# Gates of two retention heads as jobs of seven products ahead of the retention, and output projections moved into the next head

## The chip, the cores and the metric

The kernel runs on one core of one Trainium2 chip. The metric is the device time of one execution in microseconds (us); the time before is the median of three runs. PE is TensorE (matmul), DVE is VectorE, ACT is ScalarE, POOL is GpSimd, SP is SyncE, which issues most of the DMAs.

## The reference

One inference step of a two-layer decoder on 512 prompt tokens and 8 x 4 sample tokens, together T = 544 columns. The kernel keeps activations transposed, so D_MODEL = 1024 is eight tiles of 128 partitions. Layer 0 mixes with a gated short convolution, layer 1 with multi-scale retention; each is followed by a SwiGLU feed-forward.

```python
def retention_mixer(x, s0, pos, w_in, gn_g, w_out):
    z = x @ w_in                       # x: rmsnorm of the residual
    q, k, v, g = jnp.split(z, ...)     # widths 1024, 1024, 2048, 2048; 4 heads
    q = rotary(q, pos); k = rotary(k, pos) * (HEAD_DK ** -0.5)
    o, S = retention_chunkwise(q, k, v, s0)
    of = (o - mean(o)) * lax.rsqrt(var(o) + GN_EPS)       # per head
    out = (jax.nn.silu(g) * (of * gn_g)) @ w_out
    return out, S

# a layer
x = x + mixer(rmsnorm(x, norm_mix[i]))
x = x + swiglu(rmsnorm(x, norm_ffn[i]), w_gate, w_up, w_down)
```

A head has 256 key and 512 value dimensions, so a head's gate is four blocks of 128 rows (n = 0 to 3), and its output projection multiplies a 512 x 1024 part of `w_out` and adds to all eight residual tiles.

## The kernel before

**Split products.** Every float32 operand is split into a high part and the rest (`split`, lines 186 to 190: a copy on ACT, a subtraction on DVE), and each product is made as three matmuls: high by high, high by rest, rest by high. `project` (L173) makes one 128-row output block of 544 columns in two halves of 272 (HT): per 128 rows of the contraction 3 x 2 matmuls. Weights come by `load_piece` (512 KB, on SP) into a pool of three buffers and are split into `wh` and `wl`.

**Feed-forward.** `ffn` makes gate and up in jobs (`class Job`): two output blocks by two token halves by two halves of the contraction are a 2 x 2 product of blocks, which is made with seven products in place of eight, from sums of weight blocks (`weights7`, L434 to L437 on DVE, with accumulating DMAs on POOL in `mixed`, L422) and sums of activation blocks (`operands_left`, `operands_rest`, tiles `oh` and `ol`). The results are gathered in tiles `gu` (`summed`). `run` goes through the jobs: each one's weights are prepared a job ahead. The down projection (`down`) adds to the residual tiles `x` (`residual`, L269), and for layer 0 it makes the split input `xh`, `xl` of the next layer at the end (`split_x`), and sums squares on ACT and POOL (`square_sum`). `rms_scale` turns the sums into R, the reciprocal norm per token (the norm's scale is applied to results).

**Retention.** After the feed-forward's pools are closed, `qk_first` makes the first head's two key blocks and its first query block, scales and rotates them (`qk_rotate`; cosine and sine are held in `sqacc` and `sqlast`). Then, for each head h:

- `value`: 96 + 96 products of 512 columns, with the splits of queries and keys (`qk_split`), sample scores (L1090) and key transposes in the middle;
- `gate_project` for n = 0 to 3, set between the state products (`state`) and the scores (`scores`): `project`, then R on DVE (L1011), Silu and the gain on ACT;
- `sample_outputs` and `states_update` for four pieces of the sample state S (1 MB each, three buffers; loaded at L1106, updated at L1137, written at L1138), `inner` products, `normalized`, and `gated_pair`, which multiplies the gate tile in place;
- the next head's keys and queries (`qk_start`, `qk_project`) between these;
- `out_project` (heads 0 and 1): splits the gated tiles (`gated_parts`) and makes 8 x 24 matmuls. Head 2's projection is made within head 3 (`held_parts`, `held_project`), together with head 3's own (`last_project`).

Tiles that share a tag in a pool share memory, and a later one waits until the earlier one has been read. The order on each engine is set by a scheduler that works from the written order and its own estimates; `tc.issue_after` pins single steps. PSUM has two double banks (`mm`) and four single banks (`sm`).

Of the kernel before, what the change touches and what calls it, by code (L numbers as in the profile page):

```python
# [12 lines left out]
P = 128  # L13
D = 1024
KT = D // P
# [23 lines left out]
MADE = [0, 4, 2, 6, 3, 7, 1, 5]  # L39
RD = [(r, dt) for r in range(2) for dt in range(2)]  # L40
# [7 lines left out]
def hybrid_decode_kernel(ctx: ExitStack, tc: tile.TileContext, a: dict, o: dict):  # L48
# [408 lines left out]
    class Job:  # L457
# [3 lines left out]
        def __init__(self, srcs, oh, ol, sw, take):  # L461
            self.srcs, self.oh, self.ol, self.sw, self.take = srcs, oh, ol, sw, take

        lead = False
# [5 lines left out]
        def product(self, out, which, first):  # L470
            wh, wl = self.w[which]
            at, n = OPERAND[which], len(self.oh)
            for k in range(n):
                c = slice(k * P, (k + 1) * P)
                for i, (w, b) in enumerate(((wh, self.oh), (wh, self.ol), (wl, self.oh))):
                    last = nc.tensor.matmul(  # L476
                        out, w[:, c], b[k][:, at, :],
                        start=(first and k == 0 and i == 0), stop=(k == n - 1 and i == 2),
                        skip_group_check=True,
                    )  # L480
                if which not in (5, 6, 2):
                    with tc.issue_after(last.ins):
                        next(self.weave, None)
# [6 lines left out]
        def middle(self):  # L490
            for which in (5, 6) if self.lead else (6, 5):
# [3 lines left out]
                else:  # L495
                    self.c = bank()[:, :HT]
                    self.product(self.c, 5, True)
            self.b = bank()[:, :HT]
            self.product(self.b, 2, True)
            self.take("c11", self.b)  # L500
# [10 lines left out]
    def run(jobs, after, steps):  # L511

        jobs[0].lead = True
# [30 lines left out]
    def ffn(layer, next_gain):  # L544
        with ExitStack() as c1:
# [5 lines left out]
            ohl = [  # L551
                [(lp if i == KP - 1 else one).tile([P, 7, HT], F32R, tag=f"{t}{i}", name=nm(t)) for t in ("oh", "ol")]
                for i in range(KP)
            ]
            oh, ol = zip(*ohl)
# [26 lines left out]
            def gate_up(m):  # L582
# [17 lines left out]
                def up(what, src):  # L600
# [5 lines left out]
                    elif what == "c12":  # L606
# [5 lines left out]
                        [a["ffgu"][layer, 2 * j + q] for j in (m, m + HJ)], oh, ol, sw,  # L612
# [66 lines left out]
            run(jobs, after, steps)  # L679
# [5 lines left out]
            if layer == 1:  # L685
                final(last, group_acts(last), group_weights, fp, tp)

# [83 lines left out]
    ffn(0, lambda kt: g_mix(1, kt))  # L771


    with ExitStack() as c2:
        wide("m")
        vp = c2.enter_context(tc.tile_pool(name="rtv", bufs=1, reuse_waits="tile"))
        tp = c2.enter_context(tc.tile_pool(name="rt", bufs=2, reuse_waits="tile"))
# [38 lines left out]
        def qk_start(h):  # L816
# [5 lines left out]
            st["rot"] = [  # L822
                tp.tile([P, 2, T], F32, tag=f"rot{w}", name=nm("rot"), bufs=1) for w in range(2)
            ]
            return st

        def qk_first(st):

            steps = rms_scale(True, [bank(), bank()])
            ws = [load_piece(a["rtqk"][0, 2 + dt], KT * P) for dt in range(2)]  # L830
            pts = [psum() for _ in ws]
            for part in (MADE[:KP], MADE[KP:]):
                for (wh, wl), pt in zip(ws, pts):
                    first = part[0] == MADE[0]
                    project(pt, wh, wl, 0, xh, xl, first, not first, ks=part, weave=iter(()) if first else steps)
            qw, qpt = load_piece(a["rtqk"][0, 0], KT * P), [bank(), bank()]
            project(qpt, *qw, 0, xh, xl, weave=steps)
            drain(steps)
            for i, t in enumerate((cos, sin)):
                nc.sync.dma_start(t, a["rope"][i])  # L840
            for which in (1, 0):
                qk_scale(st, which)
                for dt in range(2 if which else 1):
                    qk_rotate(st, which, dt, pts[dt] if which else qpt)
# [17 lines left out]
        def qk_rotate(st, which, dt, pt):  # L862
# [4 lines left out]
            if dt == 0:  # L867
                return
# [509 lines left out]
```

## Time and profile before

| | |
|---|---|
| median of 3 runs | 1461.56 us (1461.03 to 1461.72) |
| profiled execution, its own time | 1460.43 us |
| its span | 1458.4 us |
| PE busy | 1444.1 us, 10920 matmuls |
| DVE, ACT, POOL busy | 956.2, 631.3, 130.5 us |
| mean granted PE clock | 0.998 |
| DMA | 189.62 MB, 130 GB/s over the span |

The profile is one execution. A span begins with the first instruction and ends with the last; the time of an execution has some 2 us around it. In a timeline row the first number is the start in us from the span's start, the second how long the row lasts; `x` at its end counts merged instructions, and brackets give idle time before it with what ended it. In a row of groups come busy us and the mean ns of one instruction, then the idle time before them. A row of waits gives the total in us, how many waits, and the longest. Successive instructions of an engine overlap slightly in the record, so a mean duration is a little longer than the distance from one to the next.

### The profile page before, as it was taken

Reading aid. Unit: us, or ns where it says so; the run is one execution under the profiler, and the core shown is the slowest. Engines: PE = TensorE matmul, PEld = TensorE weight load, DVE = VectorE, ACT = ScalarE, POOL = GpSimd, SP = SyncE. Lnnn points to the kernel's source line nnn. Section 1 sums busy time; section 2 is a strip of 40 time slices with the busy share of each in tenths; the row PEclk is TensorE's granted clock in tenths of the full one; section 3 lists DMA queues with packets and bytes.
Section 4 is the critical chain, followed back from the end, with each engine's and each line's share of the span. In section 5 each row is a group of like instructions: output and inputs, shape, how many; then the busy total and the mean of one; then the engine's idle time right before and its main releaser. Section 6 shows DMA issues by size and latency. Waiting matters only on the chain.

```text
span 1458.4 us, 26223 instructions
## 1 busy us (share of the span) xinstructions
PE 1444.1 (99%) x10920; PEld 1374.5 (94%) x10920; DVE 956.2 (66%) x1483; ACT 631.3 (43%) x920; POOL 130.5 (9%) x171
## 2 busy tenths in 40 slices
PE   9999999999999999999999999999999999999997
PEld 9999999999999999897988988878899999999997
DVE  5644679848749656648645934855699847749654
ACT  6222467626536435242142224133376626536434
POOL 0100011101101003000000000000011101101002
PEclk9999999999999999999999999999999999999999
DMA  6222246635546435336235613723656635536432
GB/s 227 77 91 94 90 102 152 151 109 131 131 109 144 120 82 188 109 116 236 98 116 173 203 47 116 256 101 127 175 119 148 152 109 131 134 109 145 117 80 83
DMA packets 80694, 189.62 MB, mean 130 GB/s; under 512 B 7728, under 2 KB 25008, under 8 KB 80576
## 3 DMA queue, kind: packets, MB, share of 16 engines
q1 hardware_dynamic: 66576, 162.01, 34.6%
q0 software_dynamic: 13136, 24.72, 10.2%
q8 instruction: 85, 1.39, 0.4%
q10 hardware_dynamic: 864, 1.22, 0.2%
q14 instruction: 33, 0.27, 0.1%
HBM read 166.75 MB, written 21.18 MB: 129 GB/s over the span
## 4 chain that ended last, share of the span: by engine, by line
PE 92%; DVE 5%; ACT 1%; DMA 1%; POOL 1%; issue 0%; DVEq 0%; SPq 0%; ACTq 0%; POOLq 0%
PE mm L173 39%; PE sm L476 31%; PE sm L173 7%; PE sm L897 2%; PE sm L898 2%; PE sm L899 2%; PE sm L161 2%; PE sm L163 1%; PE sm L162 1%; DVE S L1137 1%; PE sm L1116 1%; PE mm L904 1%; DVE wl L189 0%; DVE x L269 0%; PE mm L1068 0%
## 5 line engine op out<-in xcount | busy, mean ns | idle before, releaser
L188 ACT ACTIVATE wh<-w 128x1024 fp32r<-128x1024 f32 (+4 forms) x139 | 129.6, 936 | 358.0 <-PE mm L173 224.5
L173 PE MATMUL mm<-xh,wh 128*128 128x272 f32 x1020 | 213.1, 290 | 1.6 <-DVE S L1137 1.0
L173 PE MATMUL mm<-xh,wl 128*128 128x272 f32 x1020 | 210.7, 289 | 0.0
L173 PE MATMUL mm<-xl,wh 128*128 128x272 f32 x1020 | 210.0, 287 | 0.1
L476 PE MATMUL sm<-oh,wh 128*128 128x272 f32 x704 | 203.4, 289 | 1.1 <-ACT g L535 0.9
L476 PE MATMUL sm<-ol,wh 128*128 128x272 f32 x704 | 202.8, 288 | 0.0
L476 PE MATMUL sm<-oh,wl 128*128 128x272 f32 x704 | 202.4, 288 | 0.0
L189 DVE TENSOR_TENSOR wl<-w,wh 128x1024 fp32r<-128x1024 f32 (+4 forms) x139 | 150.2, 1085 | 28.2 <-ACT wh L188 25.7
L173 PEld LDWEIGHTS mm<-xh,wh 128*128 128x128 f32 x1020 | 159.9, 188 | 7.3 <-DVE wl L189 3.4
L173 PEld LDWEIGHTS mm<-xl,wh 128*128 128x128 f32 x1020 | 159.6, 188 | 0.3 <-DVE xl L201 0.3
L173 PEld LDWEIGHTS mm<-xh,wl 128*128 128x128 f32 x1020 | 159.0, 188 | 0.2
L269 DVE TENSOR_TENSOR x<-x,mm 128x544 f32<-128x544 f32 x88 | 63.3, 719 | 139.8 <-PE mm L173 139.8
L476 PE MATMUL sm<-oh,h 128*128 128x272 f32 x528 | 152.2, 288 | 0.5 <-ACT oh L188 0.5
L476 PE MATMUL sm<-oh,l 128*128 128x272 f32 x528 | 151.6, 288 | 0.0
L476 PE MATMUL sm<-ol,h 128*128 128x272 f32 x528 | 151.6, 287 | 0.0
L476 PEld LDWEIGHTS sm<-oh,wh 128*128 128x128 f32 x704 | 132.2, 188 | 1.9 <-ACT g L535 1.5
L422 POOL DMA_DIRECT2D wl<-in_ffgu_dram x88 | 75.5, 858 | 641.1 <-ACT wl L421 287.4
L476 PEld LDWEIGHTS sm<-oh,wl 128*128 128x128 f32 x704 | 132.8, 189 | 0.0
L476 PEld LDWEIGHTS sm<-ol,wh 128*128 128x128 f32 x704 | 132.2, 188 | 0.2 <-DVE ol L189 0.2
L419 ACT ACTIVATE wh<-w 128x1024 fp32r<-128x1024 f32 x88 | 93.3, 1060 | 73.9 <-PE sm L476 48.7
L476 PEld LDWEIGHTS sm<-oh,h 128*128 128x128 f32 x528 | 99.4, 188 | 1.1 <-ACT oh L188 0.9
L476 PEld LDWEIGHTS sm<-oh,l 128*128 128x128 f32 x528 | 99.4, 188 | 0.0
(259 smaller groups left out, 2976.1 us busy)
## 6 DMA issues: line engine op xcount, KB each, us to landing
w<-in_ffgu_dram SPq DMA_DIRECT2D x88, 512.0 KB, 3.9
wl<-in_ffgu_dram POOLq DMA_DIRECT2D x88, 256.0 KB, 4.8
w<-in_ffdn_dram SPq DMA_DIRECT2D x96, 192.0 KB, 2.6
S<-in_rets_dram SPq DMA_DIRECT2D x16, 1024.0 KB, 7.7
out_rets_dram<-S SPq DMA_DIRECT2D x16, 1024.0 KB, 5.4
w<-in_cvin_dram SPq DMA_DIRECT2D x21, 512.0 KB, 3.4
w<-in_rtqk_dram SPq DMA_DIRECT2D x16, 512.0 KB, 3.7
w<-in_rtv_dram SPq DMA_DIRECT2D x16, 512.0 KB, 3.6
```

What stands on the lines that cost most here:

```text
L161: nc.tensor.matmul(out, lh, rh, start=start, stop=False, skip_group_check=True)
L162: nc.tensor.matmul(out, lh, rl, start=False, stop=False, skip_group_check=True)
L173: last_product[0] = nc.tensor.matmul(half(pt, hf)[:, :HT], w[:, c], act[k][:, hf * HT : (hf + 1) * HT], start=(first and k == ks[0] and i ...
L188: h = nc.scalar.activation(dh, src, AF.Copy)
L189: last_low[0] = nc.vector.tensor_sub(dl, src, dh.bitcast(F32))
L269: last_residual[0] = nc.vector.tensor_add(xk, xk, p)
L419: nc.scalar.activation(wh, w, AF.Copy)
L422: nc.gpsimd.dma_start(wl[:, n:], src[:, n:], accum_op=ALU.add)
L476: last = nc.tensor.matmul(out, w[:, c], b[k][:, at, :], start=(first and k == 0 and i == 0), stop=(k == n - 1 and i == 2), skip_group_chec ...
L897: nc.tensor.matmul(out, xh[kt][:, ts_], wh[:, cw], start=(kt == 0), stop=False)
L898: nc.tensor.matmul(out, xh[kt][:, ts_], wl[:, cw], start=False, stop=False)
L899: nc.tensor.matmul(out, xl[kt][:, ts_], wh[:, cw], start=False, stop=(kt == KT - 1))
```

## The change

1. `ffn` gets a last step, `ahead`, inside its pools. It holds what `qk_first` did up to the products (the rms scale, two key blocks and one query block of head 0), but copies the raw results to SBUF and stores them in DRAM (`qk_made`). Then it makes the gates of heads 1 and 2 (`AHEAD`) in four jobs of seven products, two blocks each, with operands for the four sums only (products 1, 2 and 3 read `xh` and `xl`), and stores the finished gates in DRAM (`gate_made`). Stores are issued by ACT.
2. `qk_loaded` loads keys and query of head 0 back, with the decay table `gt` and the rope tables, and scales and rotates them; the second query block is made as before.
3. Heads 1 and 2 have no `gate_project`. In its four places (`fill`) they make the output projection of the head before, two residual tiles each (`held_project`). Its split operands (`held_parts`) are made within `value` and lie in the tiles `gt`, `rot1` and one of two tiles of four blocks that change places from head to head (`swapped`). The gate is loaded from DRAM behind the last of the four.
4. `out_project` is gone; heads 0, 1 and 2 end after the next head's queries. Head 3 is as before.
5. `Job` takes its operands by a function and the order of its middle products by a list; some tiles move to a pool of their own (`rtq`).

```diff
+AHEAD = (1, 2)
...
-        def __init__(self, srcs, oh, ol, sw, take):
+        def __init__(self, srcs, operand, sw, take):
...
-    ffn(0, lambda kt: g_mix(1, kt))
+    qk_made = [dram.tile([P, 2, T], F32, tag=f"qk{w}", name=nm("qkm")) for w in range(2)]
+    gate_made = {h: dram.tile([P, 4, T], F32, tag=f"g{h}", name=nm("gm")) for h in AHEAD}
+
+    def ahead(tp, fp, sw, operand_tiles):
+        wide("m")
+        steps = rms_scale(True, [bank(), bank()])
...
+        def off(which, dt, pt):
+            each(lambda p, d: nc.scalar.activation(d, p, AF.Copy), pt, halves(made[which][:, dt, :]))
+            if which:
+                if dt:
+                    nc.scalar.dma_start(qk_made[1], made[1])
+            else:
+                nc.scalar.dma_start(qk_made[0][:, dt, :], made[0][:, dt, :])
...
+        sums = {}
+        for i, k in enumerate(MADE[::2]):
+            f = fp.tile([P, 4, HT], F32, tag="f", name=nm("f"))
+            for j in range(2):
+                kt = k + j * KP
+                nc.scalar.activation(f[:, 2 * j : 2 * j + 2, :], halves(x[kt]), AF.Copy, scale=g_mix(1, kt))
+            b11, b12, b21, b22 = [f[:, j, :] for j in range(4)]
+            nc.vector.tensor_sub(b11, b12, b11)
+            nc.vector.tensor_sub(b12, b22, b12)
+            nc.vector.tensor_sub(b22, b22, b11)
+            nc.vector.tensor_sub(b21, b21, b22)
+            sums[k] = operand_tiles((i + 1) % KP, 4)
+            split(*sums[k], f)
...
+                elif what == "c12":
+                    r = R.rearrange("p a b -> p (a b)").unsqueeze(1).to_broadcast([P, 2, T])
+                    nc.vector.tensor_mul(g, g, r)
+                    nc.scalar.activation(g, g, AF.Silu)
+                    for i in range(2):
+                        nc.scalar.activation(g[:, i, :], g[:, i, :], AF.Copy, scale=g_ret(h * 4 + n + i))
+                    nc.scalar.dma_start(gate_made[h][:, n : n + 2, :], g)
...
+        jobs = [gates(h, n) for h in AHEAD for n in (0, 2)]
+        jobs[0].prepare()
+        run(jobs, (2, 5, 6), lambda i: None, iter(()))
+
+    ffn(0, lambda kt: g_mix(1, kt), ahead)
...
-        def qk_first(st):
+        def qk_loaded(st):
+            loads = [
+                (st["rot"][1], qk_made[1]), (cos, a["rope"][0]), (sin, a["rope"][1]),
+                (st["rot"][0][:, 0, :], qk_made[0][:, 0, :]),
             ]
...
+        def swapped(second, shape, dtype, name):
+            return (tp if second else vp).tile(shape, dtype, tag="gate" if second else "vyl", name=nm(name), bufs=1)
...
                     keys(h, st)
-            v4 = tp.tile([P, 2, DV], F32R, tag="rot1", name=nm("v4"), bufs=1)
+                    if h in AHEAD:
+                        held_parts(h, older)
+            v4 = tp.tile([P, 2, DV], F32R, tag="mid", name=nm("v4"), bufs=1)
...
+        def held_parts(h, st):
+            if h in AHEAD:
+                yh = [tp.tile([P, 2, T], F32R, tag=t, name=nm("oldh"), bufs=1) for t in ("gt", "rot1")]
+                yl = swapped(h == 2, [P, 4, T], F32R, "oldl")
+                for i, t in enumerate(yh):
+                    c = slice(2 * i, 2 * i + 2)
+                    split(t, yl[:, c, :], st["gate"][0][:, c, :])
...
+            def fill(n):
+                if h in AHEAD:
+                    for i in range(2):
+                        held_project(h, (0, 4, 2, 6)[n] + i)
+                else:
+                    gate_project(h, st, n)
...
+            if h in AHEAD:
+                st["gate"] = [swapped(h == 2, [P, 4, T], F32, "gate")]
+                nc.sync.dma_start(st["gate"][0], gate_made[h])
...
-            if h < NH - 2:
-                out_project(h, st)
-            elif not more:
-                held_project(0, False)
-                held_project(1, False)
-                last_project(st)
+            if not more:
+                held_project(h, 0, False)
+                held_project(h, 1, False)
+                last_project(h, st)
```

177 lines of the change are left out of this document (100 added, 77 removed).

## The prediction

> **What bounds the kernel now.** I read the page first: which engine is busy, the granted clock, and the chain that ends last.
>
> ```profile
> span 1458.4 us, 26223 instructions
> PE 1444.1 (99%) x10920; PEld 1374.5 (94%) x10920; DVE 956.2 (66%) x1483; ACT 631.3 (43%) x920; POOL 130.5 (9%) x171
> PEclk9999999999999999999999999999999999999999
> PE 92%; DVE 5%; ACT 1%; DMA 1%; POOL 1%; issue 0%; DVEq 0%; SPq 0%; ACTq 0%; POOLq 0%
> ```
>
> PE is busy for 1444.1 of 1458.4 us at full clock and makes 92% of the chain. Next I read what PE waited for, because a busy engine can still hide waits.
>
> ```profile
> PE mm L173 <- DVE S L1137: 1.0, 1, 1.0
> ...
> PE sm L1116 <- DMA S<-in_rets_dram: 0.8, 1, 0.8
> PE mm L173 <- ACT wh L194: 0.5, 1, 0.5
> ```
>
> These are three single waits, all in the last head. So PE's instruction count sets the time, wherever the other engines keep up. Then the windows by stage (columns: stretch, its us, busy us and instructions of PE, PEld, DVE, ACT, POOL, clock, DMA share, GB/s): a stretch of the first feed-forward, then heads 0, 1 and 2, then head 3 to its end.
>
> ```profile
> 250.00:560.00 310.00, 310.00 (x2475) 309.73 (x2474) 210.63 (x317) 153.23 (x230) 31.68 (x37) 1.00 0.48 121
> ...
> 595.55:721.05 125.50, 125.42 (x859) 108.98 (x858) 80.35 (x125) 36.40 (x49) 3.26 (x5) 1.00 0.43 148
> 721.05:846.55 125.50, 125.41 (x860) 109.00 (x858) 74.53 (x112) 35.29 (x48) 3.25 (x5) 1.00 0.43 143
> 846.55:947.92 101.37, 101.30 (x667) 84.93 (x666) 56.29 (x83) 27.85 (x39) 3.24 (x5) 1.00 0.45 151
> 947.92:1060.00 112.08, 109.81 (x735) 93.35 (x734) 67.39 (x111) 42.65 (x60) 4.43 (x7) 1.00 0.42 132
> ```
>
> In the feed-forward, which already runs jobs of seven products, 2475 matmuls of 272 columns take 310.00 us: 0.1253 us each, with no gap. Heads 0 and 1 end in their own output projection and head 2 does not: 193 matmuls fewer, 24.13 us shorter, 0.125 us each. So a head may follow the one before without an output projection in between, and PE does not stall.
>
> **The change, part by part.**
>
> *Matmuls.* A gate block is 8 row tiles x 3 products x 2 halves = 48 matmuls; two heads have eight blocks, 384. A job makes two blocks with 7 x 4 x 3 = 84; four jobs, 336. So 48 x 0.1253 = **6.0 us off PE**. Everything else only moves: 192 output-projection matmuls leave the ends of heads 0 and 1 and take the gates' places in heads 1 and 2, which therefore last about 101.4 us like head 2 now, and 336 x 0.1253 = 42.1 us are put ahead of head 0.
>
> *The run-in on DVE.* The sums for the jobs' operands, 4 x (4 subtractions of 272 columns and one split of 1088), stand among the last residuals of the feed-forward, and the first job's weight sums behind them. Is there room?
>
> ```profile
> 551.00:575.00 24.00, 24.00 (x194) 24.00 (x194) 22.91 (x41) 15.87 (x24) 10.26 (x8) 1.00 0.58 195
> 575.00:595.55 20.55, 20.55 (x169) 20.55 (x168) 12.49 (x19) 5.04 (x6) 1.35 (x1) 1.00 0.57 187
> ```
> ```profile
> L189 DVE TENSOR_TENSOR wl<-w,wh 128x1024 fp32r<-128x1024 f32 x90 | 109.7, 1222 | 20.5 <-ACT wh L188 18.3
> ...
> L434 DVE TENSOR_TENSOR w<-w 128x512 f32<-128x512 f32 x44 | 30.1, 685 | 3.4 <-DMA w<-in_ffgu_dram 3.4
> ...
> L596 DVE TENSOR_TENSOR g<-g,R 128x1088 f32<-128x1088 f32 x22 | 28.4, 1291 | 2.2 <-ACT h L188 0.5
> ...
> L405 DVE TENSOR_TENSOR f<-f 128x272 f32<-128x272 f32 x8 | 3.5, 434 | 0.0
> ```
> ```profile
> 568.13 1.84 DVE L201 SCALAR_TENSOR_TENSOR xl<-x,vec,xh 128x544 fp32r<-128x544 f32 x1
> 569.89 0.71 DVE L269 TENSOR_TENSOR x<-x,mm 128x544 f32<-128x544 f32 x1
> ...
> 580.84 0.17 DVE L222 TENSOR_SCALAR rN<-sm 128x6 f32<-128x6 f32 x1
> ...
> 588.17 0.72 DVE L871 TENSOR_TENSOR rt<-rot,sqlast 128x544 f32<-128x544 f32 x1
> 588.81 0.72 DVE L873 TENSOR_TENSOR rt<-rot,sqlast 128x544 f32<-128x544 f32 x1
> ```
>
> DVE instructions that follow each other start 0.08 us before the end of the one ahead (0.72 long, 0.64 apart), so I count 0.35, 0.60, 1.14 and 1.21 us for 272, 512, 1024 and 1088 columns. The sums then cost 4 x (4 x 0.35 + 1.21) = 10.4 us. The first job's weights need four sums and a split of 512 and a split of 1024 before the third product: 4.1 us. Against these 14.5 us stand 1.1 us idle up to 575, 8.1 us idle up to 595.55, and the work that leaves the stretch (the scaling and rotation of the first keys and queries, which now follow in the head: 14 of the second window's 19 instructions and most of its 12.49 us). It fits, but it runs nearly without a break, so the order decides at single deadlines:
>
> ```profile
> 568.83 0.41 PE L173 MATMUL mm<-xh,wh 128*128 128x272 f32 x2
> ...
> 583.74 1.42 PE L227 MATMUL sm<-cb,rN 128*128 128x128 f32 x12
> ...
> 589.58 0.41 PE L173 MATMUL mm<-xh,wh 128*128 128x272 f32 x2
> ```
>
> (1) The second key block needs the PSUM pair of the last residual add 24 matmuls after 568.83, at 571.85. In the new order seven subtractions and one split (3.7 us) precede that add since the saturated stretch began; one split of x (1.8 us) is put behind it, and about 0.9 us of idling is used up. The add, which ended at 570.6, then ends at about 571.6: just in time. (2) The reciprocal scale stands behind most sums; counted on in the same way it starts at about 581.1 instead of 580.84, with PE's spread at 583.74. (3) The first gate product starts at 589.6, and the third, which needs the last operand, at 592.6; that split ends at about 586. I take **0.4 us**, between 0 and 4 (second rival).
>
> *The jobs themselves.* Weight loads, accumulating DMAs on POOL (8 more), ACT copies and DVE sums are those of the feed-forward's jobs, which run without a gap at 10.5 us each; the gate's tail (one product with R, Silu, two scalings) takes the place of the hidden layer's. The six stores to DRAM are issued by ACT behind its own results and are read 60 us and more later. **Zero**, hidden behind PE.
>
> *Entry into head 0.* Keys and queries come back from DRAM, with the decay table and the rope tables ahead of them on SP; the second query block (6.0 us of PE) still runs before the values.
>
> ```profile
> 595.55 0.40 PE L897 MATMUL sm<-wh,xh 128*128 128x512 f32 x1
> ...
> 606.52 0.40 PE L899 MATMUL sm<-wh,xl 128*128 128x512 f32 x1
> ...
> 607.73 0.29 PE L1090 MATMUL mm<-rot,rot 128*32 128x32 f32 x4
> ```
>
> The rotated tiles are due when L1090 comes, 12.2 us after the first value product. The last gate product ends 6 us before that first one. From there DVE has two scalings with R (0.6, 1.2 us), the table (1.3), a weight split (1.1), scaling of both tiles (1.9), the key rotation (6 x 0.64), the late query block (0.6) and its rotation (3.8): 14.3 us, against 18.2 us. Next are two splits and a weight split (3.4 us) for the products just after. I take **0.3 us**, between 0 and 1.5.
>
> *Heads 1 and 2: two loads on SP.* The older head's halves occupy the tiles of the next decay table (`gt`, 0.56 MB) and of the gate (1.11 MB), so SP can issue both only when the last held product is done. SP keeps its order: behind them wait a weight piece, the first S written out, and the fourth S loaded into its place.
>
> ```profile
> 786.30 4.30 SPq L1138 DMA_DIRECT2D out_rets_dram<-S  x2
> 790.73 5.34 SPq L1106 DMA_DIRECT2D S<-in_rets_dram  x2
> ```
> ```profile
> 781.90:786.30 4.40, 4.40 (x29) 1.75 (x28) 4.24 (x5) 2.21 (x3) 0.00 (x0) 1.00 0.22 49
> 786.30:800.00 13.70, 13.69 (x94) 10.31 (x94) 9.44 (x19) 1.06 (x1) 1.62 (x3) 1.00 0.91 319
> ...
> ```
> ```profile
> S<-in_rets_dram SPq DMA_DIRECT2D x16, 1024.0 KB, 7.7
> ...
> gt<-in_gtab_dram SPq DMA_DIRECT2D x4, 544.0 KB, 4.4
> ```
> ```profile
> 1025.73 1.05 PE L1116 MATMUL sm<-S,qm 128*8 128x512 f32 x8 [0.76 <-DMA S<-in_rets_dram]
> ```
>
> In head 1 the gates end at 781.9. Until S goes out at 786.3 the DMA engines are 0.22 busy, then 0.91. The two loads are 1.67 MB, at 319 GB/s 5.2 us; 3.4 us of it fits before 786.3, 1.8 us does not and delays S by as much. There is no slack now: in head 3 PE waits 0.76 us for this load. The new order has S's products five 512-column products later, (606.52 - 595.55) / 47 x 5 = 1.2 us. That leaves 0.6 us in each of two heads; bounds 0 and 5.2 - 1.2 = 4.0 each. The table itself is first used by DVE some 5 us after its issue (it lands after 4.4), with the second S update and the normalizations queued behind that use; the gate is used some 15 us after its issue. The splits of the older head (two on ACT, two of 1.21 us on DVE) move from the end of heads 0 and 1 into the next head's values: zero, since head 2 leaves DVE idle for 45 of its 101.4 us. I take **1.0 us** for both heads.
>
> [...]
>
> *Sum.* -6.0 + 0.4 + 0.3 + 1.0 = -4.3 us. The profiled execution took 1460.43 us, 2.0 us round its span; 1456.1 after the change. The median of the runs is 1.13 us above that execution: **1457.3 us**, 0.29% below 1461.56. A measurement of this kernel can tell about 0.2% (2.9 us) from no change, so the line is at 1458.6.
>
> **The rivals.**
>
> *Everything hides* (0.15): all three terms are zero, -6.0, 1455.6 us. For it: head 2's entry, with no cover, costs nothing. Against it: 571.6 against 571.85, and S's wait.
>
> *DVE overruns in the run-in* (0.12). POOL adds squares for 10.26 us of the stretch from 551 to 575, and DVE slows down under them:
>
> ```profile
> 553.85 0.69 DVE L189 TENSOR_TENSOR wl<-w,wh 128x512 fp32r<-128x512 f32 x1
> ...
> 555.78 1.23 DVE L189 TENSOR_TENSOR wl<-w,wh 128x512 fp32r<-128x512 f32 x1
> ```
>
> The same split takes 0.69 or 1.23 us. If all eight new instructions ahead of the last residual add lose 0.54 us, that add is 4.3 us later and PE waits 4.1 us: -6.0 + 4.1 + 1.3 = -0.6, 1461.0 us. Against it: POOL's adds are as many as before, so the slowing is mostly in the old durations already. [...]
>
> *S arrives late by the whole length of the loads* (0.12), the other side. If nothing of gate and table fits ahead of S, and the next table's arrival holds DVE's S update as well, each of heads 1 and 2 loses 5.2 us and more; with 0.7 for the other terms, -6.0 + 10.4 + 0.7 = +5.1, 1466.7 us. It decides from 3 us a head upwards. For it: S lands exactly when needed now. Against it: the DMA engines idle for 3.4 of the 4.4 us before S goes out, and the loads are issued there.
>
> **How the numbers follow.** The forecast has 0.61: 1457.3, its own range 1455.2 to 1459.5 (S between 0 and 1.6 a head, run-in up to 1). With the first two rivals 1454.8 to 1462.0 holds 8 in 10 and leaves out the last one and a tail. Faster by over 0.2%: 0.15 and most of 0.61, 0.70. Within: the second rival and the forecast's upper end, 0.17. Slower: 0.13.
>
> **What would show it.** In the profile after: PE instructions down by 48; a 42 us stretch of jobs between the second query block's start and the feed-forward without gaps; heads 0, 1 and 2 each about 101.4 us; PE's waits for S in heads 1 and 2 near 0.5 us each; DVE filled from 551 to 586. A wait of PE at the second key block would show the run-in too tight; waits of several us at S's products, the third case. Heads longer than 101.4 us for another reason would prove the reading by stages wrong.

## The result, and the profile after

The changed kernel takes 1465.78 us (median of 8 runs, 1464.03 to 1467.77); the kernel before, run beside it, 1461.85 us (8 runs, 1461.03 to 1462.68). The ratio is 1.0027, 95% interval 1.0016 to 1.0038: slower by 3.9 us, where 4.3 us faster was forecast. The runs lie further apart than those of before, 3.7 against 1.7 us. The profiled execution took 1464.06 us.

The page after, span and engines:

```profile
span 1462.3 us, 26286 instructions
PE 1441.9 (99%) x10872; PEld 1370.5 (94%) x10872; DVE 985.7 (67%) x1525; ACT 656.8 (45%) x960; POOL 140.7 (10%) x179
```

The 48 matmuls are gone (10920 to 10872), but PE's busy time fell by 2.2 us and not by 6.0: some of the matmuls that remain got slower. The table of PE's waits, with total, number and longest:

```profile
PE mm L175 <- DVE x L271: 3.1, 1, 3.1
PE sm L1211 <- DMA S<-in_rets_dram: 1.9, 3, 0.8
PE sm L1163 <- DVE yn L1139: 1.7, 2, 0.8
```

The first row is new and is the wait that the prediction named as the sign of a run-in too tight. PE's timeline around it:

```profile
575.45 0.49 PE L175 MATMUL mm<-xh,wh 128*128 128x272 f32 x2 [3.14 <-DVE x L271]
575.77 0.42 PE L175 MATMUL mm<-xl,wh 128*128 128x272 f32 x2
...
576.90 0.66 PE L175 MATMUL mm<-xl,wh 128*128 128x272 f32 x2
...
579.56 0.41 PE L175 MATMUL mm<-xl,wh 128*128 128x272 f32 x2
```

Two costs stand here. PE stops for 3.14 us; and soon after it goes on, pairs of matmuls come 0.45 us apart instead of 0.25, until 579.5. Between 575.45 and 580.05 are 24 matmuls, 4.60 us, where 24 x 0.1253 = 3.0 were due: 1.6 us more. The windows give the granted clock:

```profile
572.00:576.00 4.00, 0.86 (x7) 0.67 (x6) 4.00 (x6) 2.91 (x5) 1.44 (x1) 1.00 0.42 120
576.00:578.00 2.00, 2.00 (x11) 2.00 (x10) 2.00 (x4) 0.64 (x1) 0.00 (x0) 0.51 0.06 23
578.00:580.00 2.00, 2.00 (x13) 2.00 (x12) 2.00 (x6) 1.01 (x1) 0.00 (x0) 0.63 0.81 250
580.00:582.00 2.00, 2.00 (x19) 2.00 (x18) 2.00 (x4) 0.61 (x2) 0.00 (x0) 1.00 0.05 20
```

DVE is busy through all of them. Its timeline up to the late add, with POOL's adds of squares beside it:

```profile
558.97 1.50 DVE L191 TENSOR_TENSOR wl<-w,wh 128x512 fp32r<-128x512 f32 x1
560.40 0.43 DVE L820 TENSOR_TENSOR f<-f 128x272 f32<-128x272 f32 x1
560.75 1.60 DVE L819 TENSOR_TENSOR f<-f 128x272 f32<-128x272 f32 x1
...
569.47 1.88 DVE L203 SCALAR_TENSOR_TENSOR xl<-x,vec,xh 128x544 fp32r<-128x544 f32 x1
...
573.11 1.57 DVE L821 TENSOR_TENSOR f<-f 128x272 f32<-128x272 f32 x1
574.60 0.71 DVE L271 TENSOR_TENSOR x<-x,mm 128x544 f32<-128x544 f32 x1
```
```profile
558.16 1.77 POOL L220 TENSOR_TENSOR sqacc<-sqacc,sq 128x544 f32<-128x544 f32 x1 [1.40 <-ACT sq L219]
560.52 1.53 POOL L220 TENSOR_TENSOR sqacc<-sqacc,sq 128x544 f32<-128x544 f32 x1 [0.59 <-ACT sq L219]
...
572.94 1.44 POOL L220 TENSOR_TENSOR sqacc<-sqacc,sq 128x544 f32<-128x544 f32 x1 [2.17 <-ACT sq L219]
```

A subtraction of 272 columns takes 0.43 us alone and 1.57 or 1.60 beside an add on POOL. By these rows it waits for the end of that add and is not merely slower: it ends at 574.68, 0.30 us after POOL's add (574.38), the other at 562.35, again 0.30 us after POOL's (562.05), and the split of 512 columns at 560.47, 0.54 us after 559.93. All six slowed instructions of this stretch end so, 0.30 us (272 columns) or 0.54 to 0.58 us (512 and 544) behind an add. In turn, POOL's add of 572.94 ends 1.20 us after the split that DVE was running when it started (571.97 to 573.18). Residual adds, with one input in PSUM, keep their 0.42 and 0.71 us beside POOL's adds. Not every instruction with two SBUF inputs is slowed: a subtraction of 272 columns at 565.26, 0.10 us behind the start of a POOL add, took 0.43 us. The six slowed instructions from 556 to 574.6 are 5.3 us longer than their like, 2.85 us of it in three of the new subtractions (1.17, 0.54 and 1.14); in the kernel before four were, by 2.6 us. The last residual add ends at 575.31 instead of 570.60.

By stages: the jobs, then the pitch from head 0 to 1, 1 to 2 and 2 to 3 (from the first sample products of one to those of the next), and the rest; below them head 2 and the rest of the kernel before, cut at the same places:

```profile
594.75:639.42 44.67, 44.31 (x346) 43.25 (x345) 28.70 (x51) 29.93 (x48) 5.56 (x8) 1.00 0.73 195
655.82:758.19 102.37, 102.30 (x666) 85.14 (x666) 64.59 (x100) 30.19 (x40) 3.30 (x5) 1.00 0.44 149
758.19:860.51 102.32, 101.17 (x666) 84.70 (x666) 66.78 (x100) 25.98 (x33) 4.27 (x5) 1.00 0.48 166
860.51:963.23 102.72, 101.21 (x666) 84.73 (x666) 65.60 (x99) 24.82 (x32) 4.25 (x5) 1.00 0.48 165
963.23:1462.30 499.07, 486.62 (x3778) 471.36 (x3777) 339.24 (x530) 250.02 (x381) 55.37 (x63) 0.99 0.48 126
```
```profile
857.84:959.22 101.38, 101.31 (x667) 84.93 (x666) 60.38 (x92) 28.95 (x39) 3.24 (x5) 1.00 0.45 151
959.22:1458.40 499.18, 486.92 (x3778) 471.39 (x3777) 339.35 (x530) 250.17 (x381) 55.29 (x63) 0.99 0.48 126
```

| term, us | forecast | this profile |
|---|---|---|
| matmuls | -6.0 | -6.0 |
| run-in: stop 3.14, lower clock 1.6 | +0.4 | +4.7 |
| waits within the jobs: 44.67 less 0.9 for seven matmuls of the second query block, less 42.1 | 0 | +1.7 |
| entry, head 0: 102.37 - 101.38 | +0.3 | +1.0 |
| heads 1 and 2: 102.32 + 102.72 - 2 x 101.38 | +1.0 | +2.3 |
| rest | 0 | -0.1 |
| sum | -4.3 | +3.6 (span +3.9) |

### The profile page after: what moved, and what is told of

It reads as the page before. It is cut to its first block, busy times and chain, and to the rows that moved or that the text cites. A ratio compares the mean times of both kernels' runs of the same rounds, so it can differ in the third digit from the quotient of the medians.

```text
span 1462.3 us, 26286 instructions
## 1 busy us (share of the span) xinstructions
PE 1441.9 (99%) x10872; PEld 1370.5 (94%) x10872; DVE 985.7 (67%) x1525; ACT 656.8 (45%) x960; POOL 140.7 (10%) x179
## 3 DMA queue, kind: packets, MB, share of 16 engines
q8 instruction: 85, 1.39, 0.4%
## 4 chain that ended last, share of the span: by engine, by line
PE 89%; DVE 5%; DMA 3%; ACT 1%; issue 1%; POOL 1%; DVEq 0%; ACTq 0%; POOLq 0%; SPq 0%
PE mm L175 35%; PE sm L478 34%; PE sm L175 6%; PE sm L990 2%; PE sm L991 2%; PE sm L992 2%; PE sm L163 1%; PE sm L164 1%; DVE S L1232 1%; PE sm L165 1%; DMA w<-in_ffgu_dram 1%; DMA S<-in_rets_dram 1%; DMA out_rets_dram<-S 1%; DVE wl L191 1%; PE mm L997 1%
## 5 line engine op out<-in xcount | busy, mean ns | idle before, releaser
L478 PE MATMUL sm<-oh,wh 128*128 128x272 f32 x736 | 213.1, 290 | 1.1 <-ACT g L538 0.9
L478 PE MATMUL sm<-ol,wh 128*128 128x272 f32 x736 | 212.1, 288 | 0.1
L175 PE MATMUL mm<-xh,wh 128*128 128x272 f32 x892 | 188.0, 291 | 4.6 <-DVE x L271 3.1
L175 PE MATMUL mm<-xh,wl 128*128 128x272 f32 x892 | 185.0, 290 | 0.0
L175 PE MATMUL mm<-xl,wh 128*128 128x272 f32 x892 | 184.4, 288 | 0.0
L191 DVE TENSOR_TENSOR wl<-w,wh 128x1024 fp32r<-128x1024 f32 (+4 forms) x131 | 140.3, 1075 | 24.4 <-ACT wh L190 22.8
L175 PEld LDWEIGHTS mm<-xh,wh 128*128 128x128 f32 x892 | 141.0, 190 | 8.4 <-issue 3.3
L175 PEld LDWEIGHTS mm<-xl,wh 128*128 128x128 f32 x892 | 140.3, 189 | 0.2 <-DVE xl L203 0.2
L175 PEld LDWEIGHTS mm<-xh,wl 128*128 128x128 f32 x892 | 139.6, 189 | 0.2
L191 DVE TENSOR_TENSOR l<-w,h 128x1024 fp32r<-128x1024 f32 x96 | 91.4, 953 | 26.6 <-ACT h L190 26.1
```

The source lines that it names most:

```text
L175: last_product[0] = nc.tensor.matmul(half(pt, hf)[:, :HT], w[:, c], act[k][:, hf * HT : (hf + 1) * HT], start=(first and k == ks[0] and i ...
L191: last_low[0] = nc.vector.tensor_sub(dl, src, dh.bitcast(F32))
L478: last = nc.tensor.matmul(out, w[:, c], b, start=(first and k == 0 and i == 0), stop=(k == KP - 1 and i == 2), skip_group_check=True,)
```

## The experiments

Ratios are to the kernel before, run in turn on the same chip; times in us are medians.

| kernel | time | before | ratio (95%) |
|---|---|---|---|
| changed | 1465.78 | 1461.85 | 1.0027 (1.0016-1.0038) |
| hold | 1464.32 | 1462.10 | 1.0013 (1.0004-1.0021) |
| no_pool_adds | 1462.80 | 1462.10 | 1.0002 (0.9993-1.0011) |
| squares_on_dve | 1465.38 | 1462.17 | 1.0019 (1.0010-1.0028) |
| hold_part_and_gate | 1471.85 | 1462.33 | 1.0066 (1.0053-1.0078) |
| late_by_4 (of before) | 1463.26 | 1462.42 | 1.0005 (0.9996-1.0014) |
| late_by_11 (of before) | 1470.52 | 1462.42 | 1.0053 (1.0039-1.0067) |
| gate_in_two | 1466.72 | 1462.10 | 1.0034 (1.0023-1.0045) |
| no_gate_load | 1463.98 | 1462.42 | 1.0005 (0.9996-1.0014) |
| hold_and_gate | 1463.26 | 1462.10 | 1.0010 (1.0001-1.0018) |
| before_fetch_moved | 1481.58 | 1462.33 | 1.0135 (1.0120-1.0151) |
| hold_gate_fetch_moved | 1482.43 | 1462.33 | 1.0137 (1.0123-1.0151) |
| after_fetch_moved | 1467.93 | 1462.77 | 1.0030 (1.0018-1.0042) |
| hold_gate_halves | 1463.22 | 1462.77 | 1.0005 (0.9996-1.0014) |
| squares_gate_halves | 1464.31 | 1462.17 | 1.0014 (1.0005-1.0023) |
| three_causes_out | 1459.16 | 1462.77 | 0.9976 (0.9966-0.9986) |

### What made the add late

**hold**

```diff
+            with tc.issue_after(last_residual[0].ins):
+                nc.vector.tensor_sub(b11, b12, b11)
...
```

> The changed kernel, with the sixteen subtractions of the operand sums held behind the last residual add of the first feed-forward's last down projection (DVE order only). Theory A, the sums in front of that add made it late, PE waited 3.1 us and then lost about 1.6 us to a lower clock: the wait at the second key block goes, the granted clock stays 1.00 from 570 to 590, the time is 4.7 us or more below the changed kernel, about 1460.5, and its runs vary as little as those of the kernel before (under 2 us between ends, not 3.7). Rival B, DVE simply has too little time for 10.4 us of sums: the same wait of about 3 us comes back at the first gate job's products that read the sums, and the time stays at 1464 or more.

The stop at the second key block shrinks to 0.18 us and the clock stays 1.00, but PE waits later:

```profile
573.38 0.49 PE L175 MATMUL mm<-xh,wh 128*128 128x272 f32 x2 [0.18 <-DVE x L271]
594.61 0.39 PE L478 MATMUL sm<-xh,wl 128*128 128x272 f32 x1 [1.02 <-DMA wl<-in_rtg_dram]
```

By the ratios about 2 us come back where 4.7 were expected, and the two intervals overlap: theory A holds for the stop, and rival B holds a third of it, as a wait for a weight sum. The runs still lie 4.1 us apart, so the stop is not all of that spread.

**no_pool_adds**

```diff
-            (add or nc.gpsimd).tensor_tensor(sqacc[:, c], sqacc[:, c], sq[:, c], op=ALU.add)
+            if (first, last) == (0, KT - 1) or first != MADE[0]:
+                (add or nc.gpsimd).tensor_tensor(sqacc[:, c], sqacc[:, c], sq[:, c], op=ALU.add)
```

> The changed kernel without the six adds on POOL that sum the squares of x in the first feed-forward's last down projection (the norm of the retention's input is left out by that; DVE's order is the same). Theory A with contention: two-input DVE instructions that run beside these adds are lengthened by 5.3 us in all (against 2.6 us in the kernel before), so without the adds the last residual add ends by 571 to 572, PE waits under 0.5 us, the clock stays, about 1461. Rival C, contention is the same as in the kernel before and the new instructions alone (3.7 us and one 1.2 us split) make the add late: the wait stays at 2 us or more, and the time at 1463 or more.

With DVE's order the same, instruction by instruction, the same steps take:

```profile
560.64 0.43 DVE L820 TENSOR_TENSOR f<-f 128x272 f32<-128x272 f32 x1
...
567.74 0.78 DVE L203 SCALAR_TENSOR_TENSOR xl<-x,vec,xh 128x544 fp32r<-128x544 f32 x1
...
570.62 0.71 DVE L272 TENSOR_TENSOR x<-x,mm 128x544 f32<-128x544 f32 x1
```

The add ends at 571.33, PE does not stop, and the ratio falls by 0.0025, 3.6 us. This profile runs 1.1 us behind that of the changed kernel where the stretch begins (the split of 551.90 is at 552.97 here), so the add is 5.0 us earlier against it, close to the 5.3 us counted above. The seven subtractions and the split alone did fit, as forecast; beside POOL's adds they did not. The subtraction of 272 columns that took 1.60 us beside such an add (at 560.75) takes 0.43 us here (at 560.64).

**squares_on_dve**: the work kept, moved from POOL to DVE.

```diff
-  square_sum(n, tp, "gu", 4, first=order[0], last=made_in[-1])
+  square_sum(n, tp, "gu", 4, first=order[0], last=made_in[-1], add=nc.vector if layer == 0 else None)
```

> The changed kernel with the six adds of squares in the first feed-forward's last down projection done by DVE (0.64 us apart, 3.8 us in all) in place of POOL. DVE's order then has two subtractions of the sums ahead of the last residual add where seven and a split stood. Theory A with contention: DVE gains 5.3 us of lengthening and pays 3.8, so the add ends by 572.5 at the latest, PE waits under 0.7 us at the second key block, the clock keeps 1.00 from 570 to 590, and the time falls by 3 us or more, to about 1462.5, its runs closer together. Rival B (DVE is full anyway): the wait moves to the spread of the norm or to the first gate products, 2 us or more there, and the time stays at 1464 or more.

No stop, full clock at 572, no slowed instruction; but the wait has moved:

```profile
588.17 1.29 DVE L191 TENSOR_TENSOR ol<-f,oh 128x1088 fp32r<-128x1088 f32 x1 [2.09 <-ACT oh L190]
```
```profile
595.35 0.39 PE L478 MATMUL sm<-xh,wl 128*128 128x272 f32 x1 [2.32 <-DMA wl<-in_rtg_dram]
```

DVE now waits for ACT's copies, and the weight sum behind them comes 2.3 us late. Contention made the stop; without it the run-in still has no room on DVE and ACT. Theory A is right about the place, rival B about the time.

**hold_part_and_gate**: the first sum's subtractions free again, with the gate in two (below).

```diff
+            held_back = tc.issue_after(last_residual[0].ins)
+            with held_back if i else ExitStack():
+                nc.vector.tensor_sub(b11, b12, b11)
                 ...
+            with tc.issue_after(last_residual[0].ins):
                 split(*sums[k], f)
```

> The kernel with the gate in two, and with the subtractions of the first operand sum left free; only its split and the other three sums are held behind the last residual add. In the version with all of them held PE waited 1.1 us for a weight sum's load on POOL's queue and 0.8 us for a split, since DVE was full until 592. With 1.4 us of subtractions taken back ahead of the add (lengthened by POOL's adds to about 2), the add still ends before 572.5: wait there under 0.7 us, no fall of the clock, and the waits at 594 shrink by about 1 us together. About 0.5 us faster than the version with all held: 1462.8 if that runs at 1463.3. If DVE is full from end to end, the gain at 594 is lost at 572 and the time is the same.

The forecast missed by 9 us. (The 0.8 us wait for a split that it names stands at 204 us in the profile of hold, far ahead of the edit.) The add was late again, by 1.5 us for PE, and deadline (2) was missed as well: POOL's power for the norm, which runs among DVE's sums in this order, took 6.08 us (1.61 in hold, second fence), and PE waited 4.25 us for it at a lower clock afterwards.

```profile
584.97 6.08 POOL L225 TENSOR_TENSOR rN<-rN,expo 128x6 f32<-128x6 f32 x1 [11.60 <-DVE rN L224]
...
591.10 2.77 PE L229 MATMUL sm<-cb,rN 128*128 128x128 f32 x12 [4.25 <-POOL rN L225]
```
```profile
583.37 1.61 POOL L225 TENSOR_TENSOR rN<-rN,expo 128x6 f32<-128x6 f32 x1 [11.95 <-DVE rN L224]
```

POOL's power ended at 591.05, 1.2 us after DVE's unbroken run of sums and splits (to 589.84). That DVE's work held POOL up here as POOL's adds hold DVE up elsewhere fits, but no run isolates it.

### What a stop of PE costs

**late_by_4** and **late_by_11**, in the kernel before (4 or 11):

```diff
+   if layer == 0 and ms[-1] == HJ - 1 and n == order[-1]:
+       for _ in range(11):
+           each(lambda p: nc.vector.tensor_scalar_mul(p, p, 1.0), pt)
    residual(n, pt)
```

> The kernel before with four multiplications by 1.0 in place (DVE, the PSUM pair of the last residual add) ahead of that add, so that it ends about 573.8 in place of 570.6 and the second key block waits about 2.0 us. Theory A (a stop of PE costs its own length, and beyond some length the granted clock falls as well): at 2 us no fall, 2 us slower, 1463.9. Rival (every stop of this kind lowers the clock): 3.6 us slower, 1465.5.

> The same with eleven multiplications: the add ends about 578.5, PE waits about 6.7 us. Theory A: the clock falls to about half for some 3.4 us in every run, 6.7 + 1.7 = 8.4 us slower, 1470.3. Rival (the clock's fall after the 3.1 us wait had nothing to do with it): 6.7 us, 1468.6, and a granted clock of 1.00 behind the wait.

With four, PE waited 0.63 us and not 2.0; the clock stayed at 1.00. That is too short a stop to tell the theories apart. With eleven:

```profile
580.40 0.79 PE L173 MATMUL mm<-xh,wh 128*128 128x272 f32 x2 [6.16 <-DVE x L269]
```
```profile
576.00:580.00 4.00, 0.00 (x0) 0.00 (x0) 3.93 (x7) 0.00 (x0) 0.00 (x0) 0.76 1.05 387
580.00:584.00 4.00, 3.60 (x16) 3.63 (x17) 2.29 (x6) 1.30 (x2) 0.00 (x0) 0.50 0.51 198
584.00:588.00 4.00, 4.00 (x32) 4.00 (x31) 0.00 (x0) 1.06 (x1) 0.00 (x0) 0.89 0.00 0
```

8.1 us slower for a stop of 6.16, in runs 0.7 us apart: theory A. The clock is at half for about 4.5 us after PE goes on. After the 3.15 us stop it fell in the profiles of the changed kernel, no_gate_load and after_fetch_moved, and not in that of gate_in_two:

```profile
575.03 0.49 PE L175 MATMUL mm<-xh,wh 128*128 128x272 f32 x2 [3.15 <-DVE x L271]
...
575.86 0.42 PE L175 MATMUL mm<-xh,wh 128*128 128x272 f32 x2
```

So a stop of this length sometimes costs 1.5 to 1.6 us more and sometimes nothing. Shorter stops can cost it too. Behind head 3's eight waits of 1.96 to 2.56 us for S (below) the clock fell in six profiles, here in hold:

```profile
1030.12 1.04 PE L1212 MATMUL sm<-S,qm 128*8 128x512 f32 x8 [2.44 <-DMA S<-in_rets_dram]
```
```profile
1030.00:1034.00 4.00, 3.88 (x21) 3.03 (x22) 2.19 (x7) 0.00 (x0) 1.06 (x2) 0.64 0.71 264
```

From the end of that wait to the end of PE's next one, for DVE's S, these six take 7.4 to 7.6 us and the other two 6.1, so a fall costs about 1.4 us there. Behind none of the waits of up to 1.56 us between 570 and 1085 us did it fall. Why the clock falls after one stop of 3.14 or 3.15 us and not after another, no run shows.

### What made S late

**gate_in_two**

```diff
-  nc.sync.dma_start(st["gate"][0], gate_made[h])
+  nc.sync.dma_start(st["gate"][0][:, :2, :], gate_made[h][:, :2, :])
   ...
+  fourth = states_load(h, st, 3)
+  if h in AHEAD:
+      with tc.issue_after(fourth.ins):
+          nc.sync.dma_start(st["gate"][0][:, 2:, :], gate_made[h][:, 2:, :])
```

> The changed kernel, with the second half of each gate (0.56 MB) loaded behind the fourth S of its head on SP instead of ahead of it. Theory: S is late by what is queued ahead of it; its waits (0.32 and 0.69 us) and those for yn behind the S updates (0.83 and 0.82 us) go or shrink below 0.3 each, 1.5 to 2.7 us off, about 1463.5. Rival D: the waits come from DVE's order (table scaling, S updates), not from SP's queue: they stay, and the time is within 0.5 us of the changed kernel.

**no_gate_load**

```diff
-  nc.sync.dma_start(st["gate"][0], gate_made[h])
+  nc.gpsimd.memset(st["gate"][0], 1.0)
```

> The changed kernel with the two loads of the finished gates (1.11 MB each, SP) replaced by a memset on POOL, so that heads 1 and 2 are gated by ones. Theory: these loads make S late; without them S lands some 3 us earlier and the waits for S and yn in heads 1 and 2 go (2.7 us), about 1463.1, or 1463.8 if some 0.3 us a head stays. Rival D (the table load, the weights and the S writes make S late by themselves): waits of 0.7 us or more stay in both heads, and the time is within 1 us of the changed kernel's.

In two, the waits for yn went and those for S stayed (0.76 and 0.69 us); the time did not fall, where 1463.5 was expected. Without the loads the one wait left in heads 1 and 2 is 0.33 us, and the ratio falls by 0.0022, 3.2 us: the gate loads are the cause of this loss and rival D falls, but moving half of each does not repair it. What goes with whole loads shows best at yn: the waits of 0.8 us stand in heads 1 and 2 of all five profiles with whole gate loads and in none without. Waits for S of 0.20 to 0.67 us occur in heads 0 to 2 of the kernel before as well (before_again, late_by_4, late_by_11), so the 0.32 and 0.69 us are only in part the change's. In both variants the scheduler put S's last products earlier again; that the waits for yn go with that order is argued from the order alone.

**before_again**: the kernel before, unchanged, profiled on the chip of these runs.

> The kernel before, once more, on the chip of these runs. In the first profile head 3 waited 0.76 us for its last S; the changed kernel and its variants waited 0.84 to 2.56 us at the same place. If that place belongs to the change, this profile shows about 0.8 again; if it varies from run to run or chip to chip, it shows 2 us or more. Heads 0 to 2: no wait for S by either theory.

It waited 0.97 us in head 3, and 0.27 and 0.20 us in heads 0 and 1, where no wait was expected. hold, no_pool_adds, gate_in_two and no_gate_load waited 2.0 to 2.6 there, with the clock falling behind the wait: something of the changed kernel, in a head that it does not change. The transfers show what. In hold, the S load's issue on SP (start, us) and, of the DMA queues in the microsecond from 1020, the one that brings PE's instructions (packets, MB, share of the 16 engines); then the issue in before_again:

```profile
1020.36 2.05 SPq L1202 DMA_DIRECT2D S<-in_rets_dram  x1
```
```profile
q8 instruction: 1, 0.02, 5.8%
```
```profile
1017.99 0.39 SPq L1106 DMA_DIRECT2D S<-in_rets_dram  x1
```

One packet of PE's instructions (85 of them, 1.39 MB, over the kernel: 16 KB each) passes as S is issued; the issue takes 2 us instead of 0.4, and in the last microseconds ahead of PE's restart, 1028 to 1030, the DMA engines move 20 GB/s.

**before_fetch_moved** and **hold_gate_fetch_moved**

```diff
-            for _ in range(WARM):
+            for _ in range(2):
                 nc.tensor.matmul(wm[:, :P], ones, ones, start=True, stop=True)
+            for _ in range(46):
+                nc.tensor.matmul(wm[:, P : P + 1], ones, ones[:, 0:1], start=True, stop=True)
```

> The kernel before with a longer warm-up: 2 matmuls of 128 columns and 46 of one column in place of 8 of 128 columns on the same tile of ones, 160 more instructions of PE at the very start, everything behind in the same order. PE's instruction fetches (16 KB each on one DMA engine, some 20 us apart) then come some 14 us earlier against the work: from 1011 and 1033 us to about 1019, into the load of head 3's last S (issued at 1018), and in head 2 to about 919, into the one issued at 918. Theory F, such a fetch makes one sixteenth of S late: head 3's wait for S becomes 2 us or more and the clock falls behind it (3 us in all), and head 2 waits too; beside that the longer warm-up costs some 1 to 4 us, seen as a later first product. Rival G, the longer wait belongs to the changed order of loads: head 3's wait stays at 0.4 to 1.0.

> The kernel with the held sums and the gate in two, with the same longer warm-up. Its fetch at 1019, beside the load of head 3's last S (issued at 1020.2), moves to about 1005 and the next from 1044 to about 1030. Theory F: head 3's wait for S falls from 2.3 to about 0.9 us or less and the clock keeps 1.00 there: 1.4 to 3 us less behind the start, against some 1 to 4 us more for the warm-up. Rival G: the wait stays at 2 us or more.

The one-column matmuls cost 0.21 us each record, 17 us at the start: only the waits can be compared. Head 3 of each:

```profile
1046.39 1.04 PE L1118 MATMUL sm<-S,qm 128*8 128x512 f32 x8 [1.96 <-DMA S<-in_rets_dram]
```
```profile
1047.77 1.04 PE L1214 MATMUL sm<-S,qm 128*8 128x512 f32 x8 [0.41 <-DMA S<-in_rets_dram]
```

The kernel before got the wait (and one of 0.82 us in head 2), the variant lost it: theory F. The clock stayed at 1.00 behind the 1.96 us, against the expectation. The variant got a wait of 3.17 us in head 1 instead, where a fetch now meets the write of that buffer.

**after_fetch_moved**

```diff
+   n = 2 if h == NH - 1 and 0 < kt < KT - 1 and c < 3 else 1
    ...
+   for j in range(n):
+       cj = slice(j * DV // n, (j + 1) * DV // n)
+       nc.tensor.matmul(out[:, cj], v[kt][:, ts_], w[:, cw][:, cj], start=first, stop=last)
```

> The changed kernel, with 60 of head 3's 192 value products of 512 columns made as two of 256 columns each: 120 more instructions of PE ahead of head 3's last S, in time that PE needs anyway, so the instruction fetch at 1021 comes some 9 us earlier (about 1012, ahead of the write of that buffer at 1017) and the next at about 1035. Theory F (a fetch beside the write or the load of S makes it late): head 3's wait for S, 2.0 to 2.6 us in five of six profiles of this family, is below 1.0, the clock stays 1.00 there, and the time falls by 1.5 to 3.2 us, to about 1463.3. Rival G (the wait comes of the changed kernel's own order of loads): it stays at 2 us or more and the time within 0.5 us of the changed kernel's.

Head 3 waited 1.00 us at full clock, as theory F has it; the time did not fall (ratio 1.0030), though 1463.3 us was expected. Over all profiles: of nine with a fetch beside the load's issue (which then takes 1.8 to 2.1 us) one waited 0.84 us and eight 1.96 to 2.56; nine without a fetch there waited 0.38 to 1.00. What it adds to the median of the changed kernel stays open; its own profile is one with the fetch and a wait of only 0.84.

### The sum

**hold_and_gate**, and with the product halves **hold_gate_halves**:

> Both edits together: the sums behind the last residual add, and the second half of each gate behind the fourth S. If the two losses are separate the gains add up: 4.7 + 2.3 = 7.0 us below the changed kernel, about 1458.8, which is 3 us or 0.2% below the kernel before. If they aren't, or if the held sums make a new wait, it stays above 1460.

> The same split of products on top of the held sums and the gate in two, the sum of what the experiments point to. From 1463.3: the wait in head 3 falls from 2.3 to about 0.9 and the clock's fall behind it goes, 1.4 to 3 us: about 1461.3, which is 0.6 to 1 us below the kernel before and within what can be told apart. If the fetch only moves to another write or load, no gain.

**squares_gate_halves**: squares on DVE, the gate in two, the product halves.

> The same with the gate in two and 60 of head 3's value products in halves, the repair of all three causes with nothing left out. The kernel with the three causes left out stood 3.6 us below the kernel before; DVE's adds may cost up to 1 us against that, and the gate loads, in two, about 1.5 to 2 (waits of 0.7 us for S in two heads). Then 1 to 1.5 us below the kernel before: 1461.3 where that runs at 1462.5; under 0.2%, so perhaps not to be told from it.

**three_causes_out**: the edits of no_pool_adds, no_gate_load and after_fetch_moved.

> The changed kernel without its three losses: no adds of squares on POOL in the first feed-forward's last down projection (the norm of the retention's input is left out by that), a memset in place of the two gate loads (heads 1 and 2 gated by ones), and head 3's products split so that the fetch misses S. If the three causes are the whole of the miss, what is left is -6.0 for the matmuls, +1.0 for the entry into head 0 and +1.7 for the waits inside the jobs, some +0.3 beside: -3.0, 1459.2 where the kernel before runs at 1462.2. If a cause is missing, it stays above 1461.

The first three missed their forecasts: 1463.26 us for 1458.8, 1463.22 for 1461.3 and 1464.31 for 1461.3. With the gate in two and the halves, head 3's wait did fall, to 0.43 and 0.58 us, but the weight sum is still 0.85 and 1.16 us late, and the second half of the gate is now late in head 2; in hold_gate_halves (in squares_gate_halves PE waits the same 1.54 us):

```profile
927.06 0.69 DVE L1172 TENSOR_TENSOR gate<-gate,mm 128x512 f32<-128x512 f32 x1 [2.85 <-DMA gate<-gm]
```
```profile
927.81 0.66 PE L1166 MATMUL mm<-cb,yn 128*128 128x128 f32 x4 [1.54 <-DVE gate L1172]
```

three_causes_out: 1459.16 us, 3.6 us below the kernel before (interval 2.0 to 5.0): what is left of the -6.0 when the three causes are out, as summed up beforehand. The gains add up within their intervals: 3.6 for POOL's adds and 3.2 for the gate loads of a distance of 7.5 us between the changed kernel and this one; the third edit alone gained nothing. But this kernel leaves work out. Of those that leave none out, the best, hold_gate_halves, cannot be told from the kernel before, and squares_gate_halves is 2 us slower: no version found beats both.

## Why the prediction was wrong

*Matmuls, -6.0: right.* 48 fewer, and three_causes_out shows the gain.

*The run-in, +0.4: the step that failed.* "The add, which ended at 570.6, then ends at about 571.6: just in time". It ended at 575.31. The new instructions were counted at their undisturbed lengths, on the argument that "POOL's adds are as many as before, so the slowing is mostly in the old durations already". What counts is how much DVE work of two SBUF inputs meets the adds, since those that were slowed ended only 0.30 to 0.58 us behind the add's end: before, residual adds (one input in PSUM) and idle time lay beside many of them, and the lengthening was 2.6 us; with subtractions there it was 5.3. For the same reason the split of x that moved behind the add gave back 0.7 us and not the 1.8 credited: POOL held up another split in its place (569.47, 1.88 us). The second rival had the place and the cause, and nearly the wait (4.1; 3.14 measured), at a chance of 0.12, but its size was in part luck: it let all eight new instructions lose 0.54 us, 4.3 in all, where three lost 2.85 and the add ended 3.7 us after the forecast's 571.6. Neither it nor the range had the clock's fall behind a stop, 1.6 us here.

*The jobs, 0: too low by 1.7 us.* PE waits once 0.36 us for DVE's sum of a gate, and its weight loads wait for ACT where one product follows another (total, number, longest, between 590 and 650):

```profile
PEld sm L478 <- ACT gate L538: 0.7, 4, 0.2
PEld sm L478 <- ACT wh L421: 0.6, 1, 0.6
```

"Without a gap", read off the feed-forward, did not carry over to jobs whose operands and weights are made at the last moment.

*Entry into head 0, +0.3: 1.0*, inside its bounds; DVE, in its splits of the rotated tiles, comes to the first sample scores some 0.8 us late.

*Heads 1 and 2, +1.0 for both: 2.3.* The waits for S came out as sized:

```profile
826.27 1.04 PE L1211 MATMUL sm<-S,qm 128*8 128x512 f32 x8 [0.32 <-DMA S<-in_rets_dram]
832.85 0.66 PE L1163 MATMUL sm<-cb,yn 128*128 128x128 f32 x4 [0.83 <-DVE yn L1139]
928.96 1.04 PE L1211 MATMUL sm<-S,qm 128*8 128x512 f32 x8 [0.69 <-DMA S<-in_rets_dram]
935.56 0.66 PE L1163 MATMUL sm<-cb,yn 128*128 128x128 f32 x4 [0.82 <-DVE yn L1139]
```

0.32 + 0.69 = 1.0; the exact agreement is luck, since the kernel before has such waits of up to 0.67 us in other profiles. That the gate loads make S late is shown for them as a whole (without them one wait of 0.33 us is left in the two heads); in which order the transfers on SP's queue pass, no run isolates. What the sum left out are the two waits for yn: S's products stand later in the new order, which the prediction booked as 1.2 us of slack for S, and the normalization of their result is late for its transpose by 0.8 us (that the order is the reason is argued, not isolated). The third rival, the only case on the slow side, had 10.4 us here and did not come about; that its 1466.7 lies near the measured 1465.78 is chance.

So the sum was short by 4.3 us in the run-in, 1.7 in the jobs and 2.0 in the heads with their entry. The second rival named the largest of these, but came to 1461.0 because it had nothing for the clock, the jobs and the waits for yn.

## What to carry to other kernels

A run-in that "just fits" on a full engine should be counted with the lengths that its instructions have beside the other engines' work, not with their shortest: here up to 1.17 us more for a DVE instruction of two SBUF inputs that meets a POOL add (of 1.44 to 2.46 us). A stop of PE of 2 to 3 us should be priced at its length and up to 1.6 us for the clock, and moving the work out of the way can only pay if the engines behind it have room, which has to be seen for each of them (here DVE, then ACT, then the weight sums). Large transfers that arrive just in time should be checked against everything else that is moved beside them, instruction fetches among it (with one beside the load's issue PE waited 1.96 to 2.56 us in eight of nine profiles).

## What the runs showed of the hardware

A subtraction of 272 columns on DVE takes 0.43 us alone and up to 1.60 beside an add on POOL; the three that were slowed ended 0.30 us behind the add's end. After a stop of 6.16 us PE's clock was at half for 4.5 us; after 3.15 us it fell in three of four profiles, after head 3's stops of 1.96 to 2.56 us in six of eight, after 1.56 us and less not. A fetch of 16 KB of instructions that meets the issue of a 1 MB load goes with 1.8 to 2.1 us of issue time instead of 0.4, and in eight of nine profiles with a wait of 2.0 to 2.6 us for the load (0.4 to 1.0 without it); moving the fetch moved the wait. A 1-column float32 matmul cost 0.21 us a record at the start, about what one of 128 columns cost there (3.65 us for 16 in the kernel before).
